# Rotary tables of a decoder block: turned by VectorE in 32 by 32 blocks and assembled by DMAs, instead of by TensorE through PSUM

## The chip, the cores and the metric

The kernel runs on one core of one Trainium2 chip. A core has five engines with queues of their own: TensorE (PE; its weight loads are PEld), VectorE (DVE), ScalarE (ACT), GpSimd (POOL) and SyncE (SP), which here only issues DMAs. An engine works its instructions in order and waits on semaphores for what others produce. The metric is device time in microseconds of one execution; the median of the runs counts.

## The reference

A residual block with two branches over 2048 positions and 1024 channels, in fp32. What the change touches is the partial rotary embedding: of each head's 128 channels the first 32 of q and k are rotated by an angle that depends on the position.

```python
ROT_DIM = HEAD_DIM // 4          # 32
def apply_partial_rope(t, cos, sin):
    half = ROT_DIM // 2
    x1 = tf[..., :half]
    x2 = tf[..., half:ROT_DIM]
    return jnp.concatenate([x1 * cos - x2 * sin, x2 * cos + x1 * sin, tf[..., ROT_DIM:]], axis=-1)

def reference(x, c, positions, ...):
    inv_freq = ROPE_THETA ** (-jnp.arange(0, ROT_DIM, 2, dtype=jnp.float32) / ROT_DIM)
    ang = positions.astype(jnp.float32)[..., None] * inv_freq
    cos = jnp.cos(ang)[:, :, None, :]
    sin = jnp.sin(ang)[:, :, None, :]
    ...
    h = rms_norm(x, g_norm[l]) * (1.0 + scale[:, None, :]) + shift[:, None, :]
    proj = h @ w_in[l]
    x_rnn, z_rnn, q, k, v, z_attn, g_r, g_a = jnp.split(proj, IN_SPLITS, axis=-1)
    # branch A: causal convolution, gated linear recurrence (RG-LRU), silu gate, projection
    # branch B: dilated window attention in three configurations, merged, silu gate, projection
    qh = apply_partial_rope(q.reshape(B, S, N_HEADS, HEAD_DIM), cos, sin)
    kh = apply_partial_rope(k.reshape(B, S, N_HEADS, HEAD_DIM), cos, sin)
    ...
    merged = jax.nn.sigmoid(g_r + bg_r) * y_rnn + jax.nn.sigmoid(g_a + bg_a) * y_attn
    x = x + gate[:, None, :] * (merged @ w_o[l])
```

## The kernel before

**Stages.** The sequence is worked in two halves, f = 0 and f = 1, of 1024 positions. Each half first computes the values v, and then all other columns of the input projection; attention and the output projections follow when both halves are done. An fp32 factor is split into a high and a low part, and each product is three matmuls.

**Products.** The projection columns are taken in pairs of 128 and the positions of a half in two blocks of 512, and `strassen` computes the four results of such a pair by seven products instead of eight. A product is 12 matmuls of 128x512 into one of the PSUM banks X, Z, W, V, Y. `n_prod` counts them. In f = 0 the left factors S of a pair are built from raw weights (`R` tiles, loaded by SP, L256) and stored to `sD`; in f = 1 the first 20 pairs reload them from `sD` (L319), seven ahead.

**What sets the order.** This stage is ordered by hand: work beside the products is hung on product numbers (`later`, `steps_after`, `after_prod`), and `run_late` issues after product n what is hung on n. All engines see their instructions in that order. `total` (L456) adds a result out of PSUM into a tile `ev`; `gate` takes the sigmoid, multiplies and stores it (L1240, L1247, L1251, to `zaT`, `grT`, `gaT`); `plain` stores unrotated channels of q and k (L1193, to `kqT`). The tag `ev` has three slots in the pool `rp`: who writes a new `ev` tile waits until the slot's last user is done, a store included.

**The tables.** Per half, `rotary_tables` computes the angles with the positions on partitions: `an` and `co` are tiles of 128 x (8 x 16), 8 blocks of 128 positions and 16 frequencies, reduced to the range of the sine step by step from product 24 on (constant `TABLES`) and put through Sin at step 52 (L1076). The rotation wants the channels on partitions: a table of 128 rows by 1024 positions, whose rows repeat every 32 (four heads' 32 rotated channels stand in one tile), with sines negative in the first 16. So four pieces, at products 90, 94, 111 and 116 after the half's start (`PIECES`), each copy 4 blocks eight times over (`repeat`, VectorE, L1083), turn them by four 128x128 transposes on TensorE into a PSUM tile `pg` (`turn`, L1088), copy it out with the sign (`store`, by ScalarE for cosines, L1094, by VectorE for sines, L1096) and store 256 KB to the scratch `tabD` in HBM (L1097, SP). In f = 0 the tiles of a piece take `ev` slots; in f = 1 they take tiles of the ring `R`. Later `load_tables` loads the two tables Ct and St of the half, 512 KB each (L1116), for `rotated_pairs`, which multiplies by them on GpSimd (L1150) and VectorE (L1153).

Of the kernel before, what the change touches and what calls it, by code (L numbers as in the profile page):

```python
# [20 lines left out]
P = 128  # L21
# [4 lines left out]
CH = 512  # L26
# [12 lines left out]
NEG = 1e30  # L39

TABLES = 24
PIECES = (90, 94, 111, 116)

KV = (2, 3), (4, 3), (4, 3), (4, 3)

# [46 lines left out]
def decoder_block(ctx, tc, x, c, positions, g_norm, w_mod, b_mod, w_in, b_gate, conv_w, conv_b,  # L92
# [4 lines left out]
    def T(pool, shape, dt, tag, **kw):  # L97
        cnt[0] += 1
        return pool.tile(shape, dt, tag=tag, name=f"{tag}_{cnt[0]}", **kw)
# [3 lines left out]
    def scratch(name, shape):  # L103
        return nc.dram_tensor(name, shape, F32, kind="Internal").ap()
# [12 lines left out]
    meT = scratch("meT", [D, S])  # L117
    gateD = scratch("gateD", [1, D])

    tabD = scratch("tabD", [2, 2, P, HALF])  # L120

    sD = scratch("sD", [REBUILT * 7, P, 2, KH, P])

# [75 lines left out]
    def raw_tile(shape):  # L199
        i = ring["R"] % NRAW  # L200
        ring["R"] += 1
        return T(pR if i < 4 else wq, shape, F32, f"R{i}")
# [833 lines left out]
    def rotary_tables(rp, f):  # L1036
# [23 lines left out]
        def reduce(per, bits, n):  # L1060
            yield tensor("kk", "an", float(1 / per), None, ALU.mult)
            yield tensor("kk", "kk", magic, None, ALU.add)
            yield tensor("kk", "kk", -magic, None, ALU.add)
            for cc in split_const(per, bits, n):
                yield lambda cc=cc: nc.vector.scalar_tensor_tensor(flat("an"), flat("kk"), -cc, flat("an"), ALU.mult, ALU.add)
# [6 lines left out]
                   *(tensor(tag, tag, lim, -lim, ALU.min, ALU.max) for tag in ("an", "co")))  # L1072

        def sines():
            for tag in ("an", "co"):
                nc.scalar.activation(flat(tag), flat(tag), AF.Sin)  # L1076

        def piece(q, i):

            def repeat():  # L1080
                src = v[("co", "an")[i]]
                v["rep"] = raw_tile([P, 4, 8, 16]) if f else T(rp, [P, 4, 8, 16], F32, "ev", bufs=3)
                nc.vector.tensor_copy(v["rep"][:], src[:, 4 * q : 4 * q + 4, :].unsqueeze(2).broadcast_to([P, 4, 8, 16]))  # L1083

            def turn():
                v["pt"] = T(pg, [P, 4, P], F32, "pg")
                for r in range(4):
                    nc.tensor.transpose(v["pt"][:, r, :], v["rep"][:, r].rearrange("p a b -> p (a b)"), ident)  # L1088

            def store():  # L1090
                t = raw_tile([P, CH]) if f else T(rp, [P, CH], F32, "ev", bufs=3)
                pt = v["pt"][:].rearrange("p r j -> p (r j)")
                if i == 0:
                    nc.scalar.activation(t[:], pt, AF.Copy)  # L1094
                else:
                    nc.vector.tensor_scalar(t[:], pt, cs[:, K_SG : K_SG + 1], None, ALU.mult)  # L1096
                nc.sync.dma_start(tabD[f, i, :, q * CH : (q + 1) * CH], t[:])  # L1097

            return repeat, turn, store

        at_, base = TABLES, n_prod[0]
        for fn in (angles, None, convert, products, *reduce(TWO_PI * 4096, 7, 8), *reduce(TWO_PI, 11, 5), *quarter, None, sines):
            if fn:
                after_prod.setdefault(base + at_, []).append(fn)
            at_ += 1
        assert at_ <= PIECES[0]

        for x, (q, i) in enumerate((q, i) for q in range(2) for i in range(2)):
            for d, fn in zip((0, 2, 3), piece(q, i)):
                after_prod.setdefault(base + PIECES[x] + d, []).append(fn)  # L1110

    def load_tables(qp, f):
        Ct = T(qp, [P, HALF], F32, "Ct")
        St = T(qp, [P, HALF], F32, "St")
        for i, t in enumerate((Ct, St)):
            later(1 + i, lambda i=i, t=t: nc.sync.dma_start(t[:], tabD[f, i]))  # L1116
        return Ct, St

    swap = [(i + 16) % 32 for i in range(32)]
# [1096 lines left out]
```

## Time and profile before

| what | us |
|---|---|
| median of 3 runs | 2173.12 |
| lowest and highest run | 2172.37, 2176.79 |
| span of the profiled execution, first to last instruction | 2175.5 |
| PE busy in it | 2144.2 (99%) |
| DVE, ACT, POOL busy | 1503.7, 1296.3, 1112.1 |
| transposes on L1088, f = 0 | 392.9 to 469.0 in the span |
| transposes on L1088, f = 1 | 1049.8 to 1125.1 |
| loads of Ct and St | 577.7 and 578.3; 1231.3 and 1232.2 |

For the profiled execution no time beside the span was taken; the span lies inside the scatter of the three runs. A row of a timeline reads: start, duration, engine, line, operation, tiles written <- tiles read, count, and in brackets the idle time before it with what ended it. SPq is SP issuing a DMA. In lists of an operation the three numbers are the shortest, median and longest in ns. The row of a window gives, per engine, busy us (instructions), then the TensorE clock, the busy share of the DMA engines and GB/s.

### The profile page before, as it was taken

The page shows a single profiled execution, that of the slowest core. Times are in us where ns is not written, and L with a number is a line of the kernel's source. Part 1 is how long each engine was busy: PE and PEld are TensorE (multiplying, and loading weights), DVE is VectorE, ACT ScalarE, POOL GpSimd, SP SyncE. Part 2 cuts the span into 40 slices and gives each one's busy share as a digit, 9 for nine tenths or more (in the row PEclk, how much of TensorE's full clock was granted, in tenths as well). Part 3 has the DMA queues.
Part 4 walks back from the last instruction along what each step waited for, and adds up shares of the span by engine and source line. Part 5 has one row for each costly group of instructions (what it writes and reads, how often), then busy time and mean ns, then how long its engine had stood idle before and what let it go on. Part 6 is the DMA issues. An engine that isn't in the chain of part 4 may idle for free.

```text
span 2175.5 us, 32647 instructions
## 1 busy us (share of the span) xinstructions
PE 2144.2 (99%) x10570; PEld 1792.5 (82%) x10571; DVE 1503.7 (69%) x2600; ACT 1296.3 (60%) x2591; POOL 1112.1 (51%) x868
## 2 busy tenths in 40 slices
PE   9999999999999999999999999999999999999998
PEld 6888788888788888888888887888888988878886
DVE  6759877868656725545446584587777787688887
ACT  5748668658644527457448532677877877444333
POOL 1467677667666323223224664466665574422444
PEclk9999999999999999999999999999999999999999
DMA  8467887886655378899996666888886777899553
GB/s 300 144 208 261 278 300 268 287 282 240 174 112 165 110 246 284 293 311 307 326 324 221 164 161 198 275 274 265 267 263 211 255 229 231 296 320 297 186 170 112
DMA packets 413040, 522.98 MB, mean 240 GB/s; under 512 B 103142, under 2 KB 278466, under 8 KB 411844
## 3 DMA queue, kind: packets, MB, share of 16 engines
q1 hardware_dynamic: 372852, 403.22, 59.6%
q10 hardware_dynamic: 34384, 99.78, 12.3%
q0 software_dynamic: 5632, 17.88, 2.6%
q8 instruction: 84, 1.38, 0.3%
q14 instruction: 88, 0.72, 0.1%
HBM read 332.02 MB, written 188.75 MB: 239 GB/s over the span
## 4 chain that ended last, share of the span: by engine, by line
PE 61%; DVE 6%; DMA 3%; ACT 2%; issue 1%; POOL 1%; SPq 0%; POOLq 0%; DVEq 0%; ACTq 0%
PE X L153 11%; PE pj L153 11%; PE V L153 11%; PE Z L153 6%; PE W L153 6%; PE Y L153 5%; PE sc L153 4%; PE o L153 4%; PE pT L1571 1%; PE pg L153 1%; PE pT L1584 1%; DVE ptl L170 1%; DVE pp L1485 1%; DVE yh L164 1%; ACT pp L1486 1%
## 5 line engine op out<-in xcount | busy, mean ns | idle before, releaser
L167 POOL TENSOR_TENSOR S<-R,S 128x512 fp32r<-128x512 f32 x192 | 296.7, 1553 | 176.9 <-ACT S L161 85.9
L153 PE MATMUL X<-T,S 128*128 128x512 f32 x1344 | 324.0, 390 | 3.1 <-ACT u L386 2.6
L153 PE MATMUL pj<-yh,S 128*128 128x512 f32 x896 | 325.8, 405 | 0.0
L153 PE MATMUL V<-T,S 128*128 128x512 f32 x1344 | 324.2, 390 | 0.2 <-DVE ev L456 0.2
L153 PEld LDWEIGHTS X<-T,S 128*128 128x128 f32 x1344 | 251.6, 188 | 58.0 <-ACT u L386 4.3
L153 PEld LDWEIGHTS V<-T,S 128*128 128x128 f32 x1344 | 251.9, 188 | 53.9 <-DVE ev L456 0.8
L167 POOL TENSOR_TENSOR S<-s,S 128x512 fp32r<-128x512 f32 x116 | 170.5, 1470 | 145.7 <-ACT S L161 109.4
L153 PEld LDWEIGHTS pj<-yh,S 128*128 128x128 f32 x896 | 169.5, 189 | 30.2 <-DVE S L170 0.7
L153 PE MATMUL pj<-yl,S 128*128 128x512 f32 x448 | 176.6, 394 | 0.3 <-POOL yl L167 0.3
L1486 ACT ACTIVATE pp<-pp,st 128x256 f32<-128x256 f32 (+3 forms) x256 | 133.6, 523 | 69.4 <-DVE st L1485 68.1
L161 ACT ACTIVATE S<-s 128x512 fp32r<-128x512 f32 x124 | 77.4, 624 | 146.9 <-DVE s L286 91.8
L153 PE MATMUL Z<-T,S 128*128 128x512 f32 x672 | 161.9, 390 | 0.0
L153 PE MATMUL Y<-T,S 128*128 128x512 f32 x672 | 161.8, 390 | 0.0
L153 PE MATMUL W<-T,S 128*128 128x512 f32 x672 | 161.6, 389 | 0.0
L161 ACT ACTIVATE S<-R 128x512 fp32r<-128x512 f32 x200 | 121.4, 622 | 59.8 <-DMA R<-in_w_in_dram 15.4
L170 DVE TENSOR_TENSOR ptl<-pT,pth 128x384 fp32r<-128x384 f32 (+1 forms) x160 | 97.9, 628 | 76.1 <-ACT pth L161 73.9
L153 PEld LDWEIGHTS W<-T,S 128*128 128x128 f32 x672 | 126.0, 188 | 26.9 <-issue 0.9
L153 PEld LDWEIGHTS Y<-T,S 128*128 128x128 f32 x672 | 125.9, 188 | 26.1
L153 PEld LDWEIGHTS Z<-T,S 128*128 128x128 f32 x672 | 125.9, 188 | 26.0
L975 DVE SCALAR_TENSOR_TENSOR xc<-xr,par,xc 128x512 f32<-128x512 f32 x96 | 102.5, 1068 | 56.7 <-ACT xc L969 54.4
L167 POOL TENSOR_TENSOR s<-R,s 128x512 fp32r<-128x512 f32 x32 | 43.5, 1360 | 191.0 <-ACT s L161 171.4
L1551 ACT ACTIVATE pp<-pp,M 128x256 f32<-128x256 f32 (+3 forms) x256 | 118.0, 522 | 9.9 <-DVE M L1674 9.9
(424 smaller groups left out, 4949.0 us busy)
## 6 DMA issues: line engine op xcount, KB each, us to landing
sD<-S ACTq DMA_DIRECT2D x140, 512.0 KB, 3.7
S<-sD SPq DMA_DIRECT2D x140, 512.0 KB, 5.2
S<-wD SPq DMA_DIRECT2D x82, 512.0 KB, 5.5
R<-in_w_in_dram SPq DMA_DIRECT2D x144, 256.0 KB, 3.6
wD<-s ACTq DMA_DIRECT2D x64, 256.0 KB, 4.9
kraw<-kqT SPq DMA_DIRECT2D x32, 384.0 KB, 5.5
T<-in_w_mod_dram SPq DMA_DIRECT2D x16, 512.0 KB, 8.9
vN<-ev SPq DMA_DIRECT2D x32, 256.0 KB, 2.5
```

The source lines that it names most:

```text
L153: nc.tensor.matmul(o, lhsT=l, rhs=r, start=st, stop=sp, **kw)
L161: nc.scalar.activation(o, i, AF.Copy)
L164: nc.vector.tensor_copy(o, i)
L167: nc.gpsimd.tensor_tensor(o, i, h.bitcast(F32), ALU.subtract)
L170: return nc.vector.tensor_tensor(o, i, h.bitcast(F32), ALU.subtract).ins
L975: nc.vector.scalar_tensor_tensor(xc, xr[:, i : i + CH], cw(i), xc, ALU.mult, ALU.add)
L1485: nc.vector.tensor_tensor_reduce(pdst, s_ps, mask, 1.0, 3e38, ALU.add, ALU.min, m_)
L1486: nc.scalar.activation(pdst, pdst, AF.Exp, bias=m_, scale=-1.0, accum_out=l_)
L1551: nc.scalar.activation(pp, pp, AF.Copy, scale=w)
L1571: nc.tensor.transpose(pt[:, c0 + j * P : c0 + (j + 1) * P], pp[i][:, k * P : (k + 1) * P], ident)
L1584: nc.tensor.transpose(pt[:, c * P : (c + 1) * P], pp[:, half * P : (half + 1) * P], ident)
```

## The change

The sine step (step 52) now writes four pieces into one 128x512 tile w: for each of the 8 blocks 32 columns, cosines twice, or minus sine and sine. The sign comes from the scale of the activation. At step 53 VectorE turns that tile with one instruction in 32x32 blocks: in the result t, a block of 32 positions on the partitions has become a block of 32 channels. So 32 partitions of t hold the 32 table rows for a quarter of the positions, in runs of 32 positions. At steps 54 and 55 four stores each, one for 32 partitions, put the runs where they belong in `tabD`, which now has 32 rows instead of 128: 256 runs of 128 bytes per store. `load_tables` loads the 32 rows four times, once for each 32 partitions of Ct and St. `PIECES`, the copies, the transposes and the copies out of PSUM are gone. w and t take `ev` slots in f = 0 and `R` tiles in f = 1.

```diff
@@ -39,7 +39,6 @@
 NEG = 1e30
 
 TABLES = 24
-PIECES = (90, 94, 111, 116)
 
 KV = (2, 3), (4, 3), (4, 3), (4, 3)
 
@@ -117,7 +116,7 @@
     meT = scratch("meT", [D, S])
     gateD = scratch("gateD", [1, D])
 
-    tabD = scratch("tabD", [2, 2, P, HALF])
+    tabD = scratch("tabD", [2, 2, 32, HALF])
 
     sD = scratch("sD", [REBUILT * 7, P, 2, KH, P])
 
@@ -1072,48 +1071,38 @@
                    *(tensor(tag, tag, lim, -lim, ALU.min, ALU.max) for tag in ("an", "co")))
 
         def sines():
-            for tag in ("an", "co"):
-                nc.scalar.activation(flat(tag), flat(tag), AF.Sin)
-
-        def piece(q, i):
-
-            def repeat():
-                src = v[("co", "an")[i]]
-                v["rep"] = raw_tile([P, 4, 8, 16]) if f else T(rp, [P, 4, 8, 16], F32, "ev", bufs=3)
-                nc.vector.tensor_copy(v["rep"][:], src[:, 4 * q : 4 * q + 4, :].unsqueeze(2).broadcast_to([P, 4, 8, 16]))
-
-            def turn():
-                v["pt"] = T(pg, [P, 4, P], F32, "pg")
-                for r in range(4):
-                    nc.tensor.transpose(v["pt"][:, r, :], v["rep"][:, r].rearrange("p a b -> p (a b)"), ident)
-
-            def store():
-                t = raw_tile([P, CH]) if f else T(rp, [P, CH], F32, "ev", bufs=3)
-                pt = v["pt"][:].rearrange("p r j -> p (r j)")
-                if i == 0:
-                    nc.scalar.activation(t[:], pt, AF.Copy)
-                else:
-                    nc.vector.tensor_scalar(t[:], pt, cs[:, K_SG : K_SG + 1], None, ALU.mult)
-                nc.sync.dma_start(tabD[f, i, :, q * CH : (q + 1) * CH], t[:])
-
-            return repeat, turn, store
+            w = v["w"] = (raw_tile([P, KH, P]) if f else T(rp, [P, 4, P], F32, "ev", bufs=3))[:].rearrange("p k m -> p (k m)")
+            for i, (tag, first) in enumerate((("co", 1.0), ("an", -1.0))):
+                rows = w[:, i * 2 * P : (i + 1) * 2 * P].rearrange("p (b h f) -> p b h f", b=8, h=2)
+                for h, sign in ((0, first), (1, 1.0)):
+                    nc.scalar.activation(rows[:, :, h, :], v[tag][:], AF.Sin, scale=sign)
+
+        def turn():
+            t = v["t"] = (raw_tile([P, KH, P]) if f else T(rp, [P, 4, P], F32, "ev", bufs=3))[:].rearrange("p k m -> p (k m)")
+            nc.vector.transpose(t, v["w"])
+
+        def store(i):
+            for q in range(4):
+                nc.sync.dma_start(tabD[f, i].rearrange("d (b p j) -> p d b j", b=8, p=4)[q],
+                                  v["t"][q * 32 : (q + 1) * 32, i * 2 * P : (i + 1) * 2 * P].rearrange("p (b j) -> p b j", b=8))
 
         at_, base = TABLES, n_prod[0]
-        for fn in (angles, None, convert, products, *reduce(TWO_PI * 4096, 7, 8), *reduce(TWO_PI, 11, 5), *quarter, None, sines):
+        for fn in (angles, None, convert, products, *reduce(TWO_PI * 4096, 7, 8), *reduce(TWO_PI, 11, 5), *quarter, None, sines,
+                   turn, lambda: store(0), lambda: store(1)):
             if fn:
                 after_prod.setdefault(base + at_, []).append(fn)
             at_ += 1
-        assert at_ <= PIECES[0]
-
-        for x, (q, i) in enumerate((q, i) for q in range(2) for i in range(2)):
-            for d, fn in zip((0, 2, 3), piece(q, i)):
-                after_prod.setdefault(base + PIECES[x] + d, []).append(fn)
 
     def load_tables(qp, f):
         Ct = T(qp, [P, HALF], F32, "Ct")
         St = T(qp, [P, HALF], F32, "St")
+
+        def load(i, t):
+            for hh in range(4):
+                nc.sync.dma_start(t[hh * 32 : (hh + 1) * 32, :], tabD[f, i])
+
         for i, t in enumerate((Ct, St)):
-            later(1 + i, lambda i=i, t=t: nc.sync.dma_start(t[:], tabD[f, i]))
+            later(1 + i, lambda i=i, t=t: load(i, t))
         return Ct, St
 
     swap = [(i + 16) % 32 for i in range(32)]
```

**TensorE, the first table piece of f = 0.** Rows of the order are line, operation, tile written <- tiles read, shape. V, then Z, are products (T right factors, S left factors; a product has more rows than these); `cs` holds the identity. Before:

```order
L153 MATMUL V_3603<-T_691,S_655_3559 128x512
L153 MATMUL V_3603<-T_690,S_655_3559 128x512
L1088 MATMUL pg_3721<-cs_60,ev_3674 128x128 x4
L153 MATMUL Z_3733<-T_898,S_669_3621 128x512
L153 MATMUL Z_3733<-T_899,S_669_3621 128x512
```

And now:

```order
L152 MATMUL V_3616<-T_691,S_657_3572 128x512
L152 MATMUL V_3616<-T_690,S_657_3572 128x512
L152 MATMUL Z_3739<-T_898,S_671_3634 128x512
L152 MATMUL Z_3739<-T_899,S_671_3634 128x512
L152 MATMUL Z_3739<-T_898,S_671_3634 128x512 x2
```

The four transposes between the products are gone, here and at the seven other places; nothing else on TensorE moves.

**VectorE behind step 52 of f = 0,** with the semaphores that each row waits for. u is a sum that the results share, V, Y, X the banks, sg a sigmoid, y and t the recurrence, s and R left factors; DMAHW0 to 7 are the semaphores that the DMAs of SP and ACT take in turn. Before:

```order
L392 TENSOR_TENSOR u_490_2671<-W_2637,u_483_2634 128x512 [waits PE_49]
L294 TENSOR_TENSOR R_465_2526<-R_461_2498,R_465_2526 128x512
L456 TENSOR_TENSOR ev_2699<-V_2673,u_490_2671 128x512 [waits DMAHW2_49,DMAHW0_49,DMAHW6_49,DVE_49,PE_49]
L993 SCALAR_TENSOR_TENSOR y_2686<-y_2686,sp_103_569,bigr_1231 128x512 [waits Activation_49]
L1247 SCALAR_TENSOR_TENSOR ev_2699<-sg_2715,ev_2699 128x512 [waits Activation_49]
L456 TENSOR_TENSOR ev_2752<-Y_2724,u_490_2671 128x512 [waits DMAHW5_49,DMAHW4_49,PE_49]
L1004 SCALAR_TENSOR_TENSOR t_2738<-y_2686,t_2738 128x512 [waits Activation_49]
L1247 SCALAR_TENSOR_TENSOR ev_2723<-sg_2744,X_2560 128x512 [waits DMAHW3_49,DMAHW2_49,Activation_49]
L1247 SCALAR_TENSOR_TENSOR ev_2752<-sg_2770,ev_2752 128x512 [waits Activation_49]
L299 TENSOR_TENSOR s_488_2664<-R_481_2631,s_488_2664 128x512 [waits DMAHW6_49,Pool_49]
L456 TENSOR_TENSOR ev_2796<-V_2673,u_483_2634 128x512 [waits DMAHW0_49,PE_49]
```

And now (`ev_2661` is w, `ev_2695` is t):

```order
L391 TENSOR_TENSOR u_491_2674<-W_2637,u_483_2634 128x512 [waits PE_49]
L1082 STREAM_TRANSPOSE ev_2695<-ev_2661 128x512 [waits DMAHW5_49,DMAHW4_49,Activation_49]
L293 TENSOR_TENSOR R_465_2526<-R_461_2498,R_465_2526 128x512
L455 TENSOR_TENSOR ev_2704<-V_2676,u_491_2674 128x512 [waits DMAHW2_49,DMAHW0_49,DMAHW6_49,DVE_49,PE_49]
L992 SCALAR_TENSOR_TENSOR y_2689<-y_2689,sp_103_569,bigr_1231 128x512 [waits Activation_49]
L1236 SCALAR_TENSOR_TENSOR ev_2704<-sg_2720,ev_2704 128x512 [waits Activation_49]
L455 TENSOR_TENSOR ev_2765<-Y_2733,u_491_2674 128x512 [waits DMAHW3_49,DMAHW2_49,PE_49]
L1003 SCALAR_TENSOR_TENSOR t_2747<-y_2689,t_2747 128x512 [waits Activation_49]
L1236 SCALAR_TENSOR_TENSOR ev_2732<-sg_2753,X_2560 128x512 [waits DMAHW4_49,DVE_49,Activation_49]
L1236 SCALAR_TENSOR_TENSOR ev_2765<-sg_2783,ev_2765 128x512 [waits Activation_49]
L298 TENSOR_TENSOR s_489_2667<-R_481_2631,s_489_2667 128x512 [waits DMAHW6_49,Pool_49]
L455 TENSOR_TENSOR ev_2809<-V_2676,u_483_2634 128x512 [waits DMAHW5_49,DMAHW1_49,DMAHW7_49,DMAHW0_49,PE_49]
```

The turn stands behind u<-W, and its users' slots shift: the last row, the second result out of V, waited for one DMA and now waits for four.

**SP at the same place.** A DMA waits for the last one with its semaphore and then takes that semaphore. Before:

```order
L256 DMA R_495_2697<-in_w_in_dram 128x4x128 [waits DMAHW4_49]
L256 DMA R_499_2721<-in_w_in_dram 128x4x128 [waits DMAHW5_49,DVE_49,Pool_49]
L1251 DMA zaT<-ev_2699 128x512 [waits DMAHW0_49,DVE_49]
L256 DMA R_506_2750<-in_w_in_dram 128x4x128 [waits DMAHW2_49,Pool_49]
L1251 DMA zaT<-ev_2723 128x512 [waits DMAHW5_49,DVE_49]
L1251 DMA zaT<-ev_2752 128x512 [waits DMAHW6_49,DVE_49]
```

And now:

```order
L255 DMA R_497_2702<-in_w_in_dram 128x4x128 [waits DMAHW4_49]
L1086 DMA tabD<-ev_2695 256x1x32 [waits DMAHW5_49,DVE_49]
L1086 DMA tabD<-ev_2695 256x1x32 [waits DMAHW7_49]
L1086 DMA tabD<-ev_2695 256x1x32 [waits DMAHW0_49]
L1086 DMA tabD<-ev_2695 256x1x32 [waits DMAHW1_49]
L255 DMA R_501_2730<-in_w_in_dram 128x4x128 [waits DMAHW2_49,DVE_49,Pool_49]
L1240 DMA zaT<-ev_2704 128x512 [waits DMAHW4_49,DVE_49]
L1086 DMA tabD<-ev_2695 256x1x32 [waits DMAHW5_49]
L1086 DMA tabD<-ev_2695 256x1x32 [waits DMAHW7_49]
L1086 DMA tabD<-ev_2695 256x1x32 [waits DMAHW0_49]
L1086 DMA tabD<-ev_2695 256x1x32 [waits DMAHW1_49]
L255 DMA R_508_2763<-in_w_in_dram 128x4x128 [waits DMAHW2_49,Pool_49]
```

Four short stores stand ahead of the next weight load and the first zaT store, four behind it. These last four have DMAHW5, 7, 0 and 1, for which the last row of VectorE above waits.

**SP at the same place of f = 1,** where `S` tiles are reloaded for the products. Before:

```order
L319 DMA S_1577_8568<-sD 128x1024
L319 DMA S_1581_8588<-sD 128x1024
L1251 DMA zaT<-ev_8554 128x512
L1251 DMA zaT<-ev_8574 128x512
L319 DMA S_1590_8635<-sD 128x1024
```

And now:

```order
L318 DMA S_1569_8552<-sD 128x1024
L1086 DMA tabD<-R_1566_8532 256x1x32 x4
L318 DMA S_1573_8576<-sD 128x1024
L1240 DMA zaT<-ev_8538 128x512
L1086 DMA tabD<-R_1566_8532 256x1x32 x4
L1240 DMA zaT<-ev_8562 128x512
L318 DMA S_1582_8627<-sD 128x1024
```

The short stores read an `R` tile, and stand ahead of a reload and of the first and second zaT stores.

## The prediction

> **What bounds the kernel now.** I read the page's busy lines first, then who waited for whom on TensorE, then the order of time around the table work, and last the DMA queues there.
>
> ```profile
> span 2175.5 us, 32647 instructions
> PE 2144.2 (99%) x10570; PEld 1792.5 (82%) x10571; DVE 1503.7 (69%) x2600; ACT 1296.3 (60%) x2591; POOL 1112.1 (51%) x868
> ```
>
> TensorE (PE) is busy for all but 31 us of 2175.5, so an instruction taken from it pays and one moved between the other engines does not, unless TensorE comes to wait. The waits of TensorE from 260 to 500 us, where the first half's tables are made and turned, are one line; from 850 to 1240 us, in the second half, there are none.
>
> ```profile
> PE pg L1088 <- DVE ev L1083: 0.6, 1, 0.6
> ```
>
> **What TensorE loses to the turning.** These are the transposes (each half has four groups of four), and then TensorE in order of time around the first group, the one that waits, and the last.
>
> ```profile
> L1088 PE MATMUL pg<-cs,ev x16: 270/272/329, 392.9 to 469.0; 128*128 128x128 f32 x16
> L1088 PE MATMUL pg<-cs,R x16: 270/272/273, 1049.8 to 1125.1; 128*128 128x128 f32 x16
> ...
> 387.50 2.88 PE L153 MATMUL X<-T,S 128*128 128x512 f32 x12
> 390.22 2.89 PE L153 MATMUL V<-T,S 128*128 128x512 f32 x12
> 392.95 0.60 PE L1088 MATMUL pg<-cs,ev 128*128 128x128 f32 x4
> 393.30 3.02 PE L153 MATMUL Z<-T,S 128*128 128x512 f32 x12
> 396.15 2.88 PE L153 MATMUL W<-T,S 128*128 128x512 f32 x12
> ...
> 401.59 2.88 PE L153 MATMUL X<-T,S 128*128 128x512 f32 x12
> 405.03 0.66 PE L1088 MATMUL pg<-cs,ev 128*128 128x128 f32 x4 [0.56 <-DVE ev L1083]
> 405.45 3.01 PE L153 MATMUL Y<-T,S 128*128 128x512 f32 x12
> 408.29 2.88 PE L153 MATMUL X<-T,S 128*128 128x512 f32 x12
> ...
> 1124.73 0.60 PE L1088 MATMUL pg<-cs,R 128*128 128x128 f32 x4
> 1125.09 3.02 PE L153 MATMUL X<-T,S 128*128 128x512 f32 x12
> 1127.94 2.43 PE L153 MATMUL V<-T,S 128*128 128x512 f32 x10
> ```
>
> Products overlap (2.88 long, 2.72 from start to start), so starts are compared, not durations. A product follows another after 2.72 us (387.50 to 390.22). From the first group's start to the product after next it is 396.15 - 392.95 = 3.20, so the group costs 0.48; the last gives 1127.94 - 1124.73 - 2.72 = 0.49. For the five groups between that do not wait I take 0.48 as well. In the waiting group X should have ended its turn at 401.59 + 2.72 = 404.31, and the product after next starts at 408.29: 3.98 - 2.72 = 1.26. **Sum taken from TensorE: 7 x 0.48 + 1.26 = 4.6 us.**
>
> The Trainium skill ("TensorE: Matmul & The Clock Gate", Part 4, PE-mode transpose) puts such a transpose at about 275 ns in a kernel's context. The duration agrees (272 ns), but if it were the price, 32 of them would be 8.8 us and the kernel would come to 2164. The starts say otherwise: four cost 0.48 us, 0.12 each. The sum goes by the starts.
>
> **What else goes.** Per half, four copies and two scalings on VectorE, two copies out of PSUM on ScalarE, and four 256 KB stores on SP's queue. No TensorE wait in these stretches but the one counted is put down to them, so I price their going at nothing: their cover is the back-to-back products.
>
> **What comes.** Per half: four sines of 128 x 128 elements in place of two, one 128x512 turn on VectorE, eight short stores (256 runs of 128 bytes each) and eight table loads of 32 partitions in place of two of 128. The nearest rows: the two sines; the shuffle in VectorE for the turn, with a copy that ran beside POOL as its upper end; stores of as many runs for the issue on SP.
>
> ```profile
> L1076 ACT ACTIVATE an<-an x2: 311/311/311, 280.8 to 933.2; 128x128 f32<-128x128 f32 x2
> L1076 ACT ACTIVATE co<-co x2: 294/295/296, 281.0 to 933.4; 128x128 f32<-128x128 f32 x2
> L1149 DVE STREAM_SHUFFLE t<-t x16: 714/741/762, 587.7 to 1312.7; 128x512 f32<-128x512 f32 x16
> L1083 DVE COPY ev<-co x2: 1509/1512/1514, 389.4 to 447.8; 128x512 f32<-128x512 f32 x2
> L1193 SPq DMA_DIRECT2D kqT<-ev x32: 513/608/2055, 269.5 to 1121.8; - x32
> ```
>
> So ScalarE gains 0.6 us of work, VectorE 0.74 (to 1.5; I take 0.74, since the shuffle is the row of this shape that also moves data between partitions), and SP 8 x 0.61 = 4.9 us of issue. None of this is on TensorE's path by itself. The question is what it makes late.
>
> **First half: the turn and the slots.** The turn goes in behind u<-W, and everything behind it on VectorE moves.
>
> ```profile
> 282.48 0.68 DVE L392 TENSOR_TENSOR u<-W,u 128x512 f32<-128x512 f32 x1
> 284.19 0.68 DVE L456 TENSOR_TENSOR ev<-V,u 128x512 f32<-128x512 f32 x1
> 287.26 0.34 SPq L1251 DMA_DIRECT2D zaT<-ev  x1
> 295.21 0.68 DVE L456 TENSOR_TENSOR ev<-V,u 128x512 f32<-128x512 f32 x1
> 297.55 2.88 PE L153 MATMUL V<-T,S 128*128 128x512 f32 x12
> ```
>
> The ev<-V at 295.21 is what TensorE needs: it empties the bank V that the product at 297.55 starts anew. It ends at 295.89, 1.66 us early. The turn makes it 0.74 late, the sines at worst another 0.61 where VectorE waits for ScalarE: 1.35, inside 1.66. So this costs 0; with the turn at 1.5 it would be up to 0.5.
>
> The same ev<-V now takes the slot from which the eight short stores read, and waits for the second four to land. They are issued behind the zaT store: 287.26 + 0.74 + 0.34 + 3 x 0.61 puts the eighth at 290.2. VectorE gets there at 295.95, and TensorE waits only if it starts after 297.55 - 0.68 = 296.87. The stores may take 6.7 us to land. No store of 128-byte runs is in this trace; the nearest are those to kqT, runs of 512 bytes:
>
> ```profile
> DMA to landing us min/median/max: 2.0/3.6/8.8
> ```
>
> From the median the wait is 0, from the longest 8.8 - 6.7 = 2.1. I take 0 and keep 2.1 for the range.
>
> **Second half: SP's queue.** Here the tiles come from the ring of raw weights, and no gate waits for their slot. But the first four short stores are issued ahead of a zaT store for whose landing an ev<-V already waits:
>
> ```profile
> 944.08 1.83 SPq L1251 DMA_DIRECT2D zaT<-ev  x2
> 950.15 0.69 DVE L456 TENSOR_TENSOR ev<-V,u 128x512 f32<-128x512 f32 x1 [3.98 <-DMA zaT<-ev]
> 954.36 2.88 PE L153 MATMUL V<-T,S 128*128 128x512 f32 x12
> ...
> 928.00:960.00 32.00, 32.00 (x142) 26.47 (x141) 15.37 (x21) 19.26 (x29) 5.26 (x4) 1.00 0.98 318
> ...
> q1 hardware_dynamic: 372852, 403.22, 59.6%
> ```
>
> VectorE has 954.36 - 950.15 - 0.69 = 3.5 us to spare. Issuing four stores is 4 x 0.61 = 2.4 us if SP had no gap, nothing if they fall into one. Their 1024 packets also move ahead of it, and the DMA engines are 0.98 busy here (the last column but one of the window's row). The mean packet of SP's queue is 59.6% x 2175.5 x 16 / 372852 = 56 ns over 1.08 KB; if a 128-byte packet took as much, 1024 on 16 engines are 3.6 us. Both together are 6.0, which would make TensorE wait 2.5; a shorter packet and a gap in SP's queue give 0. I take 0, since a packet of an eighth of the mean's bytes should be nearer to the low end, and keep 2.5. The reloads of operands (S<-sD) that stand behind are issued seven products, 19 us, ahead of use, and absorb that.
>
> **Table loads.** Eight 128 KB loads move the same bytes as two of 512 KB.
>
> ```profile
> 577.72 0.48 SPq L1116 DMA_DIRECT2D Ct<-tabD  x1
> 589.50 1.30 POOL L1150 TENSOR_TENSOR t<-t,Ct 128x512 f32<-128x512 f32 x1
> 1232.18 0.43 SPq L1116 DMA_DIRECT2D St<-tabD  x1
> 1245.89 0.68 DVE L1153 TENSOR_TENSOR t<-t,St 128x512 f32<-128x512 f32 x1
> ```
>
> The first reader comes 11.8 us and 13.7 us behind the issue. Six more issues at 0.48 delay the last by 2.9 us, so at the trace's longest kqT landing, 8.8, the second half's St is there at 11.7 of 13.7. The weight loads behind them are late by as much and have several products in hand. Cost 0.
>
> **The sum.** The profiled execution would go from 2175.5 to 2170.9 us. It lies 2.4 above the median of the runs, within their scatter (2172.37 to 2176.79), so against the median: 2173.12 - 4.6 = 2168.5 us, 0.21% faster. A change of under 0.2%, 4.35 us, is about what a measurement of this kernel cannot tell from none, so the forecast stands on that line.
>
> **Rivals.**
> *Short stores eat part of it.* The two waits above, between 0 and 2.1 + 2.5 = 4.6 us: 2169 to 2173, the same. For it: the saturated DMA engines and a slack of 3.5 us. Against: the stores are 32 KB each, and 768 KB less per half is stored in all.
> *Short packets are the bound (slower).* In the second half TensorE waits 2.4 + 0.064p - 3.5 us, with p ns for a 128-byte packet. This eats the whole gain from p = 90 and is slower by over 0.2% from p = 160; at 200 it is 11.7, so 2180. No row has such stores, and 160 is nearly three mean packets. The Trainium skill ("DMA: Bandwidth & Descriptors", Specifications) speaks against the change: below 512 bytes a transfer is done as read-modify-write. As two mean packets, 112 ns, that would be a wait of 6.1 and 2174.6 us.
> *Each transpose holds TensorE for its duration.* 32 x 0.272 = 8.7 us instead of 3.9, so about 2164. The starts exclude it unless records are missing.
> *The change frees nothing*, since TensorE waits later for as much: the waits that remain are mostly for engines which TensorE itself feeds, so they move along with it. 2173.
>
> **How the numbers follow.** Forecast 0.57 (0.38 of it beyond the line of 0.2%, the rest inside), partly eaten 0.22 (same), short packets the bound 0.12 (0.10 slower by over 0.2%, 0.02 same), whole duration 0.05 (faster), nothing 0.04 (same). Faster 0.43, same 0.47, slower 0.10. The range reaches from 2166, leaving out the whole-duration case, to 2174.5, the eaten gain with the scatter of runs, leaving out the slow packets.
>
> **What would show it.** Right: no transposes left between the products of the table stretches, products 2.72 us apart there, a turn of about 0.74 us, no new wait of TensorE at V near 297 and 954. Wrong: a wait of bank V for VectorE's ev, with VectorE before it idle for DMA tabD (first half) or zaT (second half), or short stores that take over 6.7 us to land.

## The result, and the profile after

The changed kernel takes 2168.84 us, median of 7 runs (2167.59 to 2172.26), against 2173.16 (2172.37 to 2177.61) for the kernel before on the same chip: a ratio of 0.9973, 95% interval 0.9963 to 0.9982. By the medians it is 4.3 us faster, by the ratio of the runs 5.9 us (3.9 to 8.0). The profiled execution took 2169.86 us, 1.9 more than its span.

From its page, the busy lines:

```profile
span 2168.0 us, 32583 instructions
PE 2138.5 (99%) x10538; PEld 1788.4 (82%) x10539; DVE 1495.3 (69%) x2590; ACT 1295.4 (60%) x2591; POOL 1111.4 (51%) x868
```

TensorE does 5.7 us less and is still busy 99% of the span. In order of time, the place where the first transposes stood, then the two turns on VectorE and the products of the second half that answer to those at 954.36 and 1127.94 before (start, duration):

```profile
387.66 2.88 PE L152 MATMUL X<-T,S 128*128 128x512 f32 x12
390.38 2.88 PE L152 MATMUL V<-T,S 128*128 128x512 f32 x12
393.10 2.88 PE L152 MATMUL Z<-T,S 128*128 128x512 f32 x12
395.82 2.88 PE L152 MATMUL W<-T,S 128*128 128x512 f32 x12
399.17 1.16 PE L152 MATMUL V<-T,S 128*128 128x512 f32 x4 [0.47 <-DVE ev L455]
...
282.64 0.70 DVE L1082 STREAM_TRANSPOSE ev<-ev 128x512 f32<-128x512 f32 x1
930.67 0.70 DVE L1082 STREAM_TRANSPOSE R<-R 128x512 f32<-128x512 f32 x1
...
946.83 0.69 DVE L455 TENSOR_TENSOR ev<-V,u 128x512 f32<-128x512 f32 x1 [4.70 <-DMA zaT<-ev]
950.31 2.88 PE L152 MATMUL V<-T,S 128*128 128x512 f32 x12
1121.95 2.88 PE L152 MATMUL V<-T,S 128*128 128x512 f32 x12
```

Products run 2.72 us apart where transposes stood, and the turn takes 0.70 us. But there is a new wait of TensorE at 399.17, at a place the prediction didn't name. It also came a little late at V near 297, which the prediction did name:

```profile
294.40 2.88 PE L152 MATMUL W<-T,S 128*128 128x512 f32 x12
297.31 3.00 PE L152 MATMUL V<-T,S 128*128 128x512 f32 x12
```

V starts 2.91 us behind W in place of 2.72, too little for the views of waits that follow. The waits between 280 and 600 us, where the first half's tables were made and turned, are in the view of waits (in total, times, longest) of the kernel before:

```profile
PE X L153 <- ACT u L386: 1.4, 1, 1.4
PE pg L1088 <- DVE ev L1083: 0.6, 1, 0.6
PE V L153 <- DVE ev L456: 0.2, 1, 0.2
```

and of the kernel after:

```profile
PE V L152 <- DVE ev L455: 0.5, 1, 0.5
```

So besides the wait that was counted, a wait of 1.4 for ScalarE's u has gone. It stood at 566 us, 100 us behind the last piece, and outside the stretch from 260 to 500 us in which the prediction listed TensorE's waits.

**A ledger by stretch.** The products are the same in all these kernels, so the start of each can be set against its start in the profile before. In the second half V at 954.36 and V at 1127.94 became 950.31 and 1121.95: 4.05 and 5.99 us earlier, so 1.94 was gained between them. The table gives this for every kernel profiled: what TensorE gained (-) or lost (+) in three stretches of the kernel before, in us. A has the turn and the stores of the first half, B its former transposes (the stretch goes on to where the lag they leave is paid), C the second half's transposes.

| kernel | A: 290 to 385 | B: 385 to 640 | C: 1045 to 1350 |
|---|---|---|---|
| changed kernel | +0.59 | -4.22 | -1.94 |
| e1 no turns | +0.57 | +3.49 | -1.94 |
| e2 claims | +0.43 | -4.15 | -1.94 |
| e3 semaphores | 0.00 | -0.44 | 0.00 |
| e4 turns added | +1.76 | +1.99 | +5.20 |
| e5 held slots | +1.63 | +2.68 | -1.95 |
| e6 no turns, first half | 0.00 | +2.68 | -0.02 |
| e7 two short-run stores | +7.01 | -5.17 | -1.93 |
| e8 two long-run stores | 0.00 | -5.15 | -1.94 |
| e9 no turns, slots held | 0.00 | +0.66 | -1.96 |
| e10 two steps | -0.01 | -5.06 | -1.94 |
| e11 eight long-run stores | +2.27 | -4.10 | -1.93 |

For the changed kernel that is -5.57. The rest of the 7.5 us between the two profiled spans lies where the programs don't differ (0.4 before 290 us, about 2.5 behind the first scores, from 1350 to 1400, 1.1 given back after 1950). Part of it is that the profiled execution before was a long one: with the same 1.9 on top of its span it took about 2177.4 us (an estimate), 4.2 above its median, and the one after 1.0 above its own. Whether the 2.5 is all chance isn't shown. The eight kernels with the change are 2.3 to 2.8 earlier there; of the four others e1 is 3.3, e3 1.0 and e6 0.7 earlier and e9 0.6 later. The ledger is read by A, B and C alone. A of e1, e7 and e11 holds some chance too: their ev<-V near 276, ahead of every change, waited 1.3 to 1.5 us for a kqT store to land, 0 to 0.5 us in the others.

Two things don't fit the prediction: B gains 4.22 where the transposes were priced at 2.7, and A loses 0.59: 0.19 at the start of V at 297.31, and 0.55 by the start of Y two products on.

### The profile page after: what moved, and what is told of

It is laid out like the page before. It is cut to its first block, busy times and chain, and to the rows that moved or that the text cites. A ratio compares the mean times of both kernels' runs of the same rounds, so it can differ in the third digit from the quotient of the medians.

```text
span 2168.0 us, 32583 instructions
## 1 busy us (share of the span) xinstructions
PE 2138.5 (99%) x10538; PEld 1788.4 (82%) x10539; DVE 1495.3 (69%) x2590; ACT 1295.4 (60%) x2591; POOL 1111.4 (51%) x868
## 3 DMA queue, kind: packets, MB, share of 16 engines
q8 instruction: 83, 1.36, 0.2%
## 4 chain that ended last, share of the span: by engine, by line
PE 66%; DVE 6%; DMA 5%; ACT 2%; issue 2%; POOL 1%; SPq 0%; POOLq 0%; ACTq 0%; DVEq 0%
PE X L152 13%; PE V L152 13%; PE pj L152 9%; PE Z L152 7%; PE W L152 7%; PE Y L152 6%; PE sc L152 4%; PE o L152 4%; PE pg L152 1%; DMA fg<-mrT 1%; PE pT L1560 1%; DMA fg<-gaT 1%; PE pT L1573 1%; DVE ptl L169 1%; DVE yl L169 1%
```

## Experiments: are the transposes the gain?

**e1**, the kernel before without its transposes:

```
-                v["pt"] = T(pg, [P, 4, P], F32, "pg")
-                for r in range(4):
-                    nc.tensor.transpose(v["pt"][:, r, :], v["rep"][:, r]..., ident)
+                v["pt"] = v["rep"]
```

> The kernel before with its 32 transposes left out: the pieces are stored as they were repeated, not turned; copies, scalings, stores and their slots stay. Theory A (the prediction's sum: the transposes' time on TensorE is the whole gain): 4.6 us faster, 2168.6, like the changed kernel. Theory B (in the first half VectorE and ScalarE lag behind because the pieces take slots of the ring ev, and TensorE pays at the X product near 566 us for whatever it gained before): only the second half's 1.95 us is kept, 2.0 to 2.7 faster in all, about 2171; the wait of X for ScalarE's u, 1.36 us before, grows to 3 or more.

Measured: ratio to the kernel before 1.0003 (0.9994 to 1.0012). Taking all transposes away gained nothing. C shows the expected 1.94, but B lost 3.49. Theory B had the loss, but not its place: the wait of X near 566 fell to 0.74, and TensorE waited 1.89 at V near 400 and 2.18 at X near 466.

**e6**, the same edit for the first half alone:

> The kernel before with the 16 transposes of its first half alone left out (the pieces are stored as they were repeated; those of the second half are turned as before). Theory A: 2.7 us faster than before. Theory B: TensorE waits at V near 399, at X near 404 and 463 and at X near 566 for what it saved; by 640 us it is no more than 0.5 us earlier than in the kernel before, or later; same time.

Measured: 1.0017 (1.0008 to 1.0026), B +2.68, with the waits where theory B put them (0.94 at V, 0.45, 2.17 and 0.76 at the three X). Theory A falls with both. But both kernels hold a repeated piece in its slot of the ring ev one product longer than before (until its scaling, not its transposes), so they also change what theory B blames.

**e9** removes that flaw. VectorE reads one column where the transposes read, and the scaling's source is another row:

```
-                v["pt"] = T(pg, [P, 4, P], F32, "pg")
-                for r in range(4):
-                    nc.tensor.transpose(v["pt"][:, r, :], v["rep"][:, r]..., ident)
+                nc.vector.tensor_copy(v["kk"][:, 0, 0:1], v["rep"][:, 0, 0, 0:1])
...
-                pt = v["pt"][:].rearrange("p r j -> p (r j)")
+                pt = bigr[:, 0:CH]
```

> The kernel before with its transposes left out and every tile of the ring ev held as long as before: where the transposes read a piece, VectorE reads one column of it; the scalings and copies read the reset row in place of PSUM, so that the tables' values are others. Theory A (the transposes' time on TensorE is gained wherever they stand): 4.6 us faster, 2.7 of it by 640 us. Theory B (in the first half VectorE and ScalarE, late through the held slots, set TensorE's pace at X near 404, 466 and 566): by 640 us at most 1 us earlier than the kernel before, the wait of X for u near 566 is 2 us or more; the second half's 1.9 us is kept: 2 to 3 us faster in all.

Measured: 0.9998 (0.9989 to 1.0007); B +0.66, C -1.96. The profile shows where the first half's gain goes. VectorE and TensorE of e9, in order of time:

```profile
456.50 0.69 DVE L456 TENSOR_TENSOR ev<-Y,u 128x512 f32<-128x512 f32 x1 [6.53 <-DMA kqT<-ev]
...
456.01 2.88 PE L153 MATMUL W<-T,S 128*128 128x512 f32 x12
459.20 2.98 PE L153 MATMUL V<-T,S 128*128 128x512 f32 x12 [0.31 <-DVE ev L456]
462.94 3.02 PE L153 MATMUL X<-T,S 128*128 128x512 f32 x12 [0.76 <-ACT u L386]
...
567.07 3.02 PE L153 MATMUL X<-T,S 128*128 128x512 f32 x12 [1.34 <-ACT u L386]
```

In the kernel before the same W is this row:

```profile
457.84 2.88 PE L153 MATMUL W<-T,S 128*128 128x512 f32 x12
```

So at 456.01 TensorE of e9 is 1.83 us ahead. VectorE isn't: as in the kernel before (455.92, shown below) it stands 6.5 us until a kqT store lands, and its ev<-Y comes at 456.50. Presumably the piece took the slot that was free, and ev<-Y must take the one behind it. V and X wait for what VectorE and ScalarE do no earlier than before, and at 566 X waits as before. This is theory B, though its numbers were off: B was to be 1 us better at most and came out 0.66 worse, the wait near 566 was to be 2 us or more and is 1.34, and of the 2 to 3 us in all the runs show 0.4 (1.5 slower to 2.4 faster).

## Experiments: the slots

**e2**, the changed kernel with the pieces' eight claims of the ring put back, each written in one column and never read:

```
+        def claim():
+            nc.vector.tensor_copy(T(rp, [P, CH], F32, "ev", bufs=3)[:, 0:1], cs[:, K_SG : K_SG + 1])
+        if f == 0:
+            for p in (90, 94, 111, 116):
+                for d in (0, 3):
+                    after_prod.setdefault(base + p + d, []).append(claim)
```

> The changed kernel, and in its first half eight more tiles taken from the ring ev at the steps where the pieces took theirs (each written in one column, never read; no transposes, no copies of size, no stores). Theory A: nothing changes, 2168.8. Theory B: VectorE waits some 6 us for a kqT store near 450 us in place of none there, the lag stays, X near 563 us waits 1.3 to 1.6 us for ScalarE's u: 2170.3.

Measured: 0.9967 (0.9955 to 0.9980), as fast as the changed kernel, and no wait of X near 563. A tile that nobody reads is free at once, so this held nothing; theory B in this form was wrong.

**e5** holds them about as long as the pieces did (take at +0, pass on to a second tile at +3, read that at +5, one column each). The first tile is held one product longer than a piece's, which the transposes read at +2, so it has the flaw of e1 and e6:

```
+            def pass_on():
+                t.append(T(rp, [P, CH], F32, "ev", bufs=3))
+                nc.vector.tensor_copy(t[1][:, 0:1], t[0][:, 0:1])
+            def read():
+                nc.vector.tensor_copy(v["kk"][:, 0, 0:1], t[1][:, 0:1])
```

> The changed kernel, and in its first half eight more tiles taken from the ring ev as the pieces took theirs and now also held as long: the first of each piece for three products, the second for two more, each written and read in one column by VectorE; no transposes, no copies of size, no stores. Theory A (the prediction's: what lies beside TensorE is free): 2168.8, no new wait. Theory B (the held slots are what made VectorE late in the first half): VectorE waits about 6 us for a kqT store near 450 us and TensorE 1.3 us or more for ScalarE's u near 563 us; 1.5 to 2.5 us slower than the changed kernel, 2170.3 to 2171.3.

Measured: 1.0012 (1.0003 to 1.0021), so about 8 us slower than the changed kernel, whose ratio is 0.9973; far more than expected. 1.0 of it lies in A, ahead of the first claim, and is a matter of the stores (below). VectorE and TensorE of e5:

```profile
460.84 0.69 DVE L455 TENSOR_TENSOR ev<-Y,u 128x512 f32<-128x512 f32 x1 [7.69 <-DMA kqT<-ev]
...
570.11 3.02 PE L152 MATMUL X<-T,S 128*128 128x512 f32 x12 [1.34 <-ACT u L385]
```

and of the kernel before and, last two rows, the changed one:

```profile
455.92 0.69 DVE L456 TENSOR_TENSOR ev<-Y,u 128x512 f32<-128x512 f32 x1 [6.57 <-DMA kqT<-ev]
...
566.40 3.04 PE L153 MATMUL X<-T,S 128*128 128x512 f32 x12 [1.36 <-ACT u L386]
...
448.75 0.69 DVE L455 TENSOR_TENSOR ev<-Y,u 128x512 f32<-128x512 f32 x1 [0.73 <-PE Y L152]
562.97 2.88 PE L152 MATMUL X<-T,S 128*128 128x512 f32 x12
```

Held slots, with no transpose, no copy of size and no store, bring back VectorE's wait for the kqT store and TensorE's 1.34 at X. That is shown. The changed kernel frees the ring of these tiles in this stretch, which fits that B gains more than the transposes' 2.7. The size isn't shown this way: B of e5 is +2.68 where e9, with slots held as long as before, has +0.66, and e1 and e6, held one product longer, have 3.49 and 2.68. How much of the 4.9 us in B between e9 and the changed kernel is due to the four copies (3.9 us on VectorE in the first half), the scalings and the stores wasn't separated.

## Experiments: the price of a transpose

**e4**, the changed kernel with 16 transposes of a constant at each of the eight old places:

```
+            for r in range(16):
+                nc.tensor.transpose(pt[:, r % 4, :], ident, ident)
...
+        for d in (92, 96, 113, 118):
+            after_prod.setdefault(base + d, []).append(again)
```

> The changed kernel, and 16 transposes of a constant 128x128 tile put between products at each of the eight places where the kernel before had four, 128 in all (their result is not used; no copies, no stores). Theory A (0.12 us each, by the starts): 15.4 us slower, 2184. Rival (each costs its duration, 0.272): 34.8 us slower, 2203.6.

Measured: 2183.53 us, 1.0039 (1.0027 to 1.0052); against the changed kernel's 0.9973 that is 14 us for 128, of which 1.2 lie in A, ahead of the first of them. One group in order of time:

```profile
1054.01 1.91 PE L1099 MATMUL pg<-cs 128*128 128x128 f32 x16
1055.67 3.01 PE L152 MATMUL Z<-T,S 128*128 128x512 f32 x12
1058.52 2.88 PE L152 MATMUL W<-T,S 128*128 128x512 f32 x12
```

1058.52 - 1054.01 - 2.72 = 1.79 for 16, 0.112 each; C says the same, (5.20 + 1.94) / 64 = 0.112. Not 0.272: between products back to back the price is the step from start to start. Where the Trainium skill ("TensorE: Matmul & The Clock Gate", Part 4, PE-mode transpose) gives about 275 ns, that is the duration here too (272 ns in the kernel before), but not what a transpose costs in this place.

## Experiments: what the changed kernel loses at the stores

In A, VectorE's ev<-V before the product V near 297 came at 296.49 in place of 295.21. As TensorE was 0.44 ahead by then, that is 1.72 against the products, over the 1.66 us of slack, and V at 297.31 was late. VectorE and ScalarE stayed 1.28 behind the kernel before until V at 399.17. The turn isn't the cause: e8 (below) has it too, and there A is 0.00. ScalarE of the changed kernel, of e8, and of e11 (both below), each with the issue of a store of S and the tanh t<-y behind it:

```profile
286.86 0.33 ACTq L279 DMA_DIRECT2D sD<-S  x1
287.23 0.63 ACT L997 ACTIVATE t<-y 128x512 f32<-128x512 f32 x1 [1.32 <-DVE ev L1236]
```

```profile
285.01 0.33 ACTq L279 DMA_DIRECT2D sD<-S  x1
286.20 0.62 ACT L997 ACTIVATE t<-y 128x512 f32<-128x512 f32 x1
```

```profile
289.10 0.34 ACTq L279 DMA_DIRECT2D sD<-S  x1
289.49 0.63 ACT L997 ACTIVATE t<-y 128x512 f32<-128x512 f32 x1 [1.35 <-DVE ev L1236]
```

The releaser named is not what the tanh needs: it reads y, which VectorE had ready before 285.2 in the changed kernel (a row at 284.44, 0.74 long). What held ScalarE is the store of S ahead of it. The programs' order, with the semaphores that each instruction waits for, before and after:

```
ACTIVATE S<-R 128x512 [waits DMAHW3]
DMA sD<-S 128x1024 [waits DMAHW7,Pool]
ACTIVATE t<-y 128x512 [waits DVE]

ACTIVATE S<-R 128x512 [waits DMAHW3]
DMA sD<-S 128x1024 [waits DMAHW3,Pool]
ACTIVATE t<-y 128x512 [waits DVE]
```

SP's and ScalarE's transfers add in turn to eight semaphores, and a transfer waits for the last one on its own. Four more stores in between move this one from a semaphore last used by an S store, long landed, to that of a kqT store issued by 282.9 (SP's queue). By the last update of its semaphore it landed at 286.78, and the held store went at 286.86.

**e3** shifts the turn alone: the kernel before with four tiny loads at that place.

> The kernel before, and in its first half four loads of 1 KB each at the place where the changed kernel issues its first four short stores (their data is not used). They only shift the turn of the eight DMA semaphores by four, so that ScalarE's store of S near 285 us needs the one that a kqT store holds, as in the changed kernel. Theory L (the semaphore's turn makes ScalarE and VectorE 1.3 us late): the tanh starts 1.0 to 1.4 later than 285.96, ev<-V at 296.2 to 296.6 in place of 295.21, and V waits up to 0.4 us; 0 to 0.6 us slower, 2173.2 to 2173.8. Rival (the added turn and sines, or the short stores themselves, made them late): ScalarE is not held and ev<-V stays at 295.2 within 0.3; 2173.2.

Measured: 1.0001 (0.9992 to 1.0009), A 0.00; the tanh started at 285.04, not held. Theory L's forecast failed, but the shift wasn't put to the test: in this execution the kqT store had landed by 284.1, 2.0 us after its issue. In all other kernels profiled it took 3.2 to 4.1 us, in the kernel before too (3.6), where no store of S waits for it.

**e7** and **e8** store each table at once, e7 in the runs of 128 bytes that the layout asks for, e8 in runs of 1 KB as the tile lies:

```
-            for q in range(4):
-                nc.sync.dma_start(tabD[f, i]....[q], v["t"][q * 32 : (q + 1) * 32, ...])
+            nc.sync.dma_start(tabD[f, i].rearrange("d (b p j) -> p d b j", b=8, p=4), ...)   # e7
+            nc.sync.dma_start(tabD[f, i].rearrange("d (x j) -> (d x) j", x=4), ...)          # e8
```

> The changed kernel with one short-run store for each table and half (1024 runs of 128 bytes) in place of four. Theory L (the eight short stores shift the DMA semaphores so that ScalarE's store near 285 us needs the one of a kqT store on its way, which makes ScalarE and VectorE 1.3 us late up to 400 us and TensorE 0.5 us late at V near 297 and 0.6 at V near 399): with two stores that store needs one long free, ScalarE's tanh starts within 0.3 us of 285.6, both waits of V go, about 1.1 us faster than the changed kernel, 2167.7. Rival (the turn and the two more sines make them late): tanh near 287, as in the changed kernel, 2168.8.

> The changed kernel with one store for each table and half in runs of 1 KB, as the tile lies (the tables' values land in other places). If short runs cost nothing on the path, as the prediction has it: within 0.5 us of the kernel with two short-run stores. Rival (the short packets hold up SP's queue): 1 us faster than that one or more, and the store's landing over 1 us shorter.

Measured: e8 0.9967 (0.9957 to 0.9977), 2166.51 us, with A 0.00 and no wait of TensorE at all between 280 and 600 us. The rival came true in both points: e8 is about 7.6 us faster than e7 by the ratios, and its four stores landed 4.2 to 5.5 us after their issue began, e7's 6.3 to 9.1 (by the last update of each one's semaphore). e7 1.0002 (0.9993 to 1.0011), no faster than the kernel before: its tanh isn't held and B is as good as e8's, but it loses 7 us in A. SP, VectorE and TensorE of e7:

```profile
285.80 0.63 SPq L1085 DMA_DIRECT2D tabD<-ev  x1
286.55 4.79 SPq L255 DMA_DIRECT2D R<-in_w_in_dram  x1
291.44 0.73 SPq L1239 DMA_DIRECT2D zaT<-ev  x1
292.22 0.56 SPq L1085 DMA_DIRECT2D tabD<-ev  x1
292.88 6.65 SPq L255 DMA_DIRECT2D R<-in_w_in_dram  x1
299.62 0.46 SPq L1239 DMA_DIRECT2D zaT<-ev  x1
...
296.02 0.69 DVE L1235 SCALAR_TENSOR_TENSOR ev<-sg,X 128x512 f32<-128x512 f32 x1 [5.05 <-DMA zaT<-ev]
301.38 0.69 DVE L455 TENSOR_TENSOR ev<-V,u 128x512 f32<-128x512 f32 x1 [2.66 <-issue]
302.22 1.19 PE L152 MATMUL V<-T,S 128*128 128x512 f32 x2 [5.42 <-DVE ev L455]
```

After a store of 1024 short runs the next issue on SP takes 4.79 and 6.65 us. The zaT store behind it is late and VectorE waits 5.05 for its slot. Then its ev<-V waits another 2.66: it takes the slot that the two short stores read, and the semaphore of the second had its last update at 301.31, 9.1 us after the issue began. TensorE waits 5.4 for VectorE. The second part is the wait that the prediction kept for its range, stores that take over 6.7 us to land; the changed kernel escapes both by storing in quarters. The number of runs isn't all that differs: the semaphore of an e7 store was updated 5 times, that of a quarter, or of an e8 store, 16 times, so a store of 1024 runs seems to be spread over fewer of the DMA engines. Which of the two makes it slow wasn't tested. The same two rows in the changed kernel (SP's queue):

```profile
287.55 0.81 SPq L255 DMA_DIRECT2D R<-in_w_in_dram  x1
288.45 0.52 SPq L1240 DMA_DIRECT2D zaT<-ev  x1
289.02 3.25 SPq L1086 DMA_DIRECT2D tabD<-ev  x4
292.37 0.56 SPq L255 DMA_DIRECT2D R<-in_w_in_dram  x1
```

Quarters can be late as well. In e4 and e5, whose stores are those of the changed kernel, ev<-V waits here, in the changed kernel (296.49) it doesn't:

```profile
297.81 0.69 DVE L455 TENSOR_TENSOR ev<-V,u 128x512 f32<-128x512 f32 x1 [1.18 <-PE W L152]
297.37 0.69 DVE L455 TENSOR_TENSOR ev<-V,u 128x512 f32<-128x512 f32 x1 [0.88 <-PE W L152]
```

The releaser named, W, signalled its end at 297.44 and 297.14. The semaphore of the eighth short store had its last update later, at 297.63 in e4 and 297.19 in e5, just ahead of these rows; in the changed kernel that was at 296.01. TensorE waited 1.22 and 1.08 at V, which is most of A there (+1.76 and +1.63). So the wait that the prediction kept for its range comes in some executions.

**e11** separates number and runs: eight stores per half as in the changed kernel, but of 1 KB runs.

> The changed kernel with its eight stores for each half kept (32 partitions each) but in runs of 1 KB, as the tile lies (the tables' values land in other places). Theory L (the number of stores, which shifts the DMA semaphores, makes ScalarE wait): ScalarE is held 1 us or more before the tanh near 287, as with eight short stores; V near 399 waits 0.5; 2168.8. Rival S (the short runs make the kqT store land late, for which ScalarE's store then waits): ScalarE not held or held under 0.5 us, no wait at V near 399, 2166.5 to 2167.

Measured: 0.9977 (0.9968 to 0.9986), 2169.09 us. The tanh was held 1.35 (ScalarE above), and V waited 1.76 near 299 and 0.52 near 401. So theory L holds here: the holding comes with eight stores and not with short runs. It is in all five kernels with eight (1.24 to 1.39 in the changed kernel, e2, e4, e5, e11) and in none of the three with two (e7, e8, e10). The kqT store doesn't land late because of the eight: it took 3.8 to 4.1 us after its issue in these five and 4.0 to 4.1 in the three with two, where no store of S waits for it. Why it took only 2.0 in e3 stays open. Part of e11's A is chance: an ev<-V at 276.62, ahead of every change, waited 1.47 for a kqT store, 0.34 in the changed kernel.

**e10** puts this together and computes the whole layer: the turned tile stored as it lies, and the short runs copied later from DRAM to DRAM, in quarters, one every second product:

```
+            nc.sync.dma_start(tabA[f, i], v["t"][:, i * 2 * P : (i + 1) * 2 * P])
+        def spread(i, q):
+            nc.sync.dma_start(tabD[f, i].rearrange("d (b p j) -> p d b j", b=8, p=4)[q],
+                              tabA[f, i, q * 32 : (q + 1) * 32, :].rearrange("p (b j) -> p b j", b=8))
...
+        for k in range(8):
+            after_prod.setdefault(base + at_ + 18 + 2 * k, []).append(lambda k=k: spread(k // 4, k % 4))
```

> The changed kernel with the tables stored in two steps: the turned tile as it lies in runs of 1 KB (two stores for each half), and from there 18 to 32 products later eight copies from DRAM to DRAM in runs of 128 bytes, one every second product. If the short runs hurt because they stand between ScalarE's, VectorE's and the gates' transfers near 285 us, this is as fast as the kernel with long runs: TensorE 5 us earlier than the kernel before by 640 us, 2166.5 in all. Rival (short runs hold the queue up wherever they stand): the loss of 1 us or more comes back at the stretch from 345 to 385 us, 2168 or more.

Measured: 2167.63 us, 0.9969 (0.9958 to 0.9980), A -0.01, B -5.06, no wait of TensorE between 280 and 600 us. In the ledger it is 1.4 us better than the changed kernel; the runs (ratio 0.9973 there) can't tell the two apart.

## Why the prediction was right, step by step

It said 2168.5 and 2168.84 came, but two of its terms were off, in opposite directions, and in part the number was luck.

- *The transposes, 4.6 by starts.* The second half's four groups were 4 x 0.48 = 1.92 and gave 1.94 in every kernel without them. The price by starts holds (0.112 each in e4), and the rival of the whole duration is out. For the first half the 2.7 holds only together with the next point: e9 takes the transposes alone and keeps none of it. Of the transposes alone in the first half, the rival "the change frees nothing", given 0.04, is what came.
- *What else goes, priced at nothing.* This is the step that failed. The argument was that no TensorE wait in these stretches but one was put down to the pieces, and the list of waits ended at 500 us. Their tiles held slots of the ring ev, VectorE waited 6.57 us for a kqT store's slot at 455.92, ScalarE and VectorE stayed late, and TensorE paid 1.36 at X and 0.21 at V, 110 us later under other names. With nothing lost at the stores, B is -5.15 (e8): 2.4 beyond the transposes' 2.7.
- *First half, the turn and the slots: taken 0, up to 2.1.* The turn took 0.70 for 0.74 and in the changed kernel's profile the short stores landed in time: no wait for tabD (in e4 and e5 there was one, with 1.22 and 1.08 at V, inside the 2.1). But the eight stores moved ScalarE's semaphores, ScalarE was held 1.32 and VectorE came 1.72 late against the products, over the slack of 1.66: V near 297 came late, which the prediction had named as a sign of being wrong, and at 399 TensorE waited 0.47. Against e8 the changed kernel lost 0.59 in A and 0.93 in B, 1.5 us: the rival "short stores eat part of it", by a mechanism it didn't have.
- *Second half, SP's queue: taken 0, up to 2.5.* Right: ev<-V waited 4.70 in place of 3.98 for zaT, inside its 3.5 us of slack, and V at 950.31 didn't wait. The 128-byte packets of the stores took 13 ns at the median in the changed kernel's trace, where the prediction took 56 as its upper end, and its rival "short packets are the bound" needed 90 to eat the gain.
- *Table loads, 0.* Right: the ledger stands still from 640 to 1045 us (-4.06 and -4.05).

In sum 4.6 + 2.4 - 1.5 = 5.5 by the terms, 5.57 in the ledger, 4.3 by the medians and 5.9 (3.9 to 8.0) by the ratio of the runs. The forecast of 4.6 came this close because an unpriced gain and an unpriced loss partly cancelled. That is luck; the price of the transposes by starts and the second half are not.

## What to carry to other kernels

Before work is priced at nothing because the bound engine doesn't wait there, look at the ring its tiles are taken from: who takes the next slot, which store that slot waits for, and whether the lag is paid far behind under another name. When DMAs are added or taken, count them between the others, too: where semaphores go round, a different transfer may come to wait on one in flight and hold its engine's whole queue. And align the same instructions of two traces by their starts, stretch by stretch: this shows gains and losses of half a microsecond which the totals hide.

## What the runs showed that was not expected

- Behind one DMA of 1024 runs of 128 bytes the next issue on its queue took 2.3 to 6.7 us (4.79, 6.65, 2.34 and 5.47 in e7); one of 256 runs is issued in 0.6 us (median of eight, 1.2 at most), and the load behind four of them in 0.5 to 0.8. The larger DMA was the worse one here, and its semaphore was updated 5 times in place of 16.
- Short runs cost little in landing when stored in quarters: from the start of the issue to the last update of the semaphore the eight stores took 3.77 us at the median in the first half and 5.05 in the second, e11's of 1 KB runs 3.03 and 4.29. The Trainium skill ("DMA: Bandwidth & Descriptors", Specifications) has transfers below 512 bytes done as read-modify-write; whether the difference of some 0.75 us comes from that no run here shows.
- A tile that is taken and never read costs its ring nothing (e2), eight that are held for two or three products cost about 7 us (e5, +2.68 in B where the changed kernel has -4.22).
- A lag of 1.3 us of VectorE and ScalarE at 287 us lasted 110 us. TensorE paid for it at V near 297 and again at V near 399, and not at the products between.
